# Memory values' second half ahead of attention, other fillers in the router, and the overflow branch one expert earlier

## The chip, the cores and the metric

The kernel runs on one core of one Trainium2 chip. The metric is the time of one execution on the device in microseconds (us), the median of three runs. A profiled execution of the same program gives the trace.

## What is computed

Two transformer blocks over 256 tokens of width 1024, in fp32. Cut to what matters here:

```python
x = x + g1 * mixed                              # block 1: latent attention and neighbourhood attention
hx2 = modulate(rmsnorm(x, norm_ffn_g), sh2, sc2)
x = x + g2 * hierarchical_moe(hx2, ...)         # 4 groups, 16 experts: one group, then two experts of it
x = rmsnorm(x, final_norm_g)
...
kv = mem_n @ w_mem_kv                           # block 2: keys and values of 256 memory tokens
k, v = jnp.split(kv, 2, axis=-1)
...
x = x + merged @ w_out
x = x + jnp.square(jax.nn.relu(h2 @ w_up)) @ w_down
```

The memory's keys and values depend on the input alone, so they can be computed at any time before block 2's cross attention.

## The kernel before

**Products.** The big weights are read once, as pieces of up to 1 MB (128 partitions x 2048 numbers). A product is made of three fp32r matmuls: a weight piece is split by ScalarE (line 207, the high part; each fourth by VectorE) and VectorE (line 208, the rest). `Stream` holds the jobs in order; `step` runs one split piece and prepares the next ones. The loads stand in one list, `plan`, and SP issues them in that order through `pump`, as tiles of SBUF come free. Tiles are handed out by `take` and handed back by `give`, first in, first out: who takes a tile waits for its last user.

**Stages around the change.** The projections of block 1 end with the job `J_nv` (the neighbourhood attention's values). The attention begins with scores of the neighbourhood heads, then the two halves of w_uq and of w_ukv; short matmuls, softmax on VectorE and ScalarE, and ROPE on GpSimd alternate. In it, line 859 in `router_const` multiplies the shift of the norm by the router's weights. The output projection `J_wo` adds to x; behind its second half stands the router.

**Router.** x is transposed by TensorE (`xa_T`, line 1037 on; an instruction of it has the helper's line 531), the logits come from the transposed x (line 1049), the norm's factor r2 from sums of squares. VectorE ranks groups and experts by comparisons of all pairs (lines 1117 to 1126) and TensorE counts each token's slot in its expert (lines 1131 to 1133). D, a 0/1 matrix of tokens by slots for four experts, follows (line 1143). `gather` (line 1181) multiplies the normalized tokens, split into xh and xlo, by D, four experts at a time, into `xg`. The normalized token is kept in `xn`; xh is ScalarE's rounding of it and xlo GpSimd's difference. While the router waits, TensorE runs pieces of `J_mv[1]`, the second half of the memory values: `fill(n)` runs n pieces of 6 matmuls (line 252), 8 pieces in all; its result goes through the tile `mvt` to DRAM (`mvd`), from which block 2 reads it.

**MoE.** 16 experts, 64 slots each. `moe_up` multiplies by gate and up weights (line 1269), `moe_down(e - 2)` follows two experts later (line 1303), and `moe_comb(p)` adds a pair of experts to the four banks of the output (line 1328). Tokens without a slot are the matter of `beyond()`, a branch that all engines pass: each loads a flag, and jumps over the branch's body when no token was left out, as with these inputs. It stands behind the down product of expert 12. The residual x is added to the four banks by `add_x` behind the last experts.

Of the kernel before, what the change touches and what calls it, by code (L numbers as in the profile page):

```python
# [9 lines left out]
F32 = mybir.dt.float32  # L10
# [11 lines left out]
NE = 16  # L22
# [67 lines left out]
def body(tc, d, out, dbg=None, stop=None):  # L90
# [87 lines left out]
    class Stream:  # L178
# [62 lines left out]

        def fine(self, job):

            while self.pos < job.end:
                job, key, a, k, kg, first, last, done = self.g[self.pos]
                s = self.prepared.pop(self.pos)
                if first:
                    job.accs = job.acc()
                for m, (hi, lo) in enumerate(job.lhs):
                    for kk in range(kg):  # L250
                        for j, (x, w) in enumerate(((hi, 0), (lo, 0), (hi, 1))):
                            T.matmul(job.accs[m], x(k + kk), s[:, w, kk, :], start=first and kk == 0 and j == 0,  # L252
                                     stop=last and kk == kg - 1 and j == 2)
                    if last:
                        job.evac(m, job.accs[m])
                    if m == len(job.lhs) - 1:
                        give(s)
                        self.pos += 1
                    yield

        def step_w(self, job, s, k, kg, first, last):
# [330 lines left out]
    J_mk = [Job(P_memk[c], 512, mlhs, ev_memk(c)) for c in range(2)]  # L592
    J_mv = [Job(P_memv[c], 512, mlhs, ev_memv(c), acc=(lambda: [bank(), bank()]) if c else None) for c in range(2)]
    for j in J_mk + J_mv[:1]:
# [159 lines left out]
    J_nv = Job(P_nv, 512, al, ev_nv)  # L754
    for j in (J_kvl, J_ql, J_nq, J_nk, J_nv):
        S.add(j)
# [110 lines left out]
    def latents():  # L867
# [36 lines left out]
        give(st["kvl"], st["kvT"])  # L904
        router_const()

# [93 lines left out]
    J_wo = [Job(P_wo[c], 512, wol, ev_wo(c)) for c in range(2)]  # L1000
    for j in J_wo + J_mv[1:]:
        S.add(j)
# [32 lines left out]
    def xa_T(c):  # L1035
        for k0, bk in transposed_pairs(lambda tt, k: x[:, tt, 512 * c + k:512 * c + 512:4], 4):
# [22 lines left out]

    xres = x  # L1060
# [7 lines left out]
    mvt[1] = take([128, 2, 512], F32, "mvt")  # L1068
    mvg = S.fine(J_mv[1])

    def fill(n):
        for _ in range(n):
            next(mvg, None)

    fill(3)
    give(oTh, oTl, gb[0])
# [6 lines left out]
    r2 = rstd_of(ss2t, 1024, "r2")  # L1083
    fill(2)
    logits(1, 0)
    logits(1, 1)
    give(xaT)
    keep(4)
    xn = take([128, 2, 1024], F32, "xn2")
    xh = take([128, 2, 1024], F32R, "xh")  # L1090
    xlo = take([128, 2, 1024], F32R, "xlo")
    keep(1)
    def fo(t):
        return t.rearrange("p (h j q) -> p h j q", h=2, j=4)

    def fi(t):
        return t.rearrange("p (h q j) -> p h j q", h=2, j=4)

    V.tensor_scalar(fo(xn[:, 0, :]), fi(x[:, 0, :]), r2[:, 0:1], None, op0=OP.mult)
# [9 lines left out]
    keep(1)  # L1109

# [55 lines left out]
    def halves(n):  # L1166
        hi, lo = take([128, 2, 1024], F32R, "xh"), take([128, 2, 1024], F32R, "xlo")
        for tt in range(2):
            A.activation(hi[:, tt], xn[:, tt], AF.Copy)
            G.tensor_tensor(lo[:, tt], xn[:, tt], hi[:, tt].bitcast(F32), op=OP.subtract)  # L1170
        xh_[n] = hi, lo

    def gather(n):

        xh, xlo = xh_[n]
        Dn = [D[n][:, tt].rearrange("p e c -> p (e c)") for tt in range(2)]
        for q in range(2):
            bks = [bank() for _ in range(2)]
            for i, (h, tt) in enumerate(((xh, 0), (xh, 1), (xlo, 0), (xlo, 1))):
                for k in range(4):  # L1180
                    T.matmul(bks[k // 2][:, 256 * (k % 2):256 * (k % 2) + 256],
                             h[:, tt, (4 * q + k) * 128:(4 * q + k + 1) * 128], Dn[tt],
                             start=(i == 0 and k % 2 == 0), stop=(i == 3), skip_group_check=True)
            for k in range(4 * q, 4 * q + 4):
                bk = bks[(k % 4) // 2][:, 256 * (k % 2):256 * (k % 2) + 256]
                if k in (0, 1, 4, 6):
                    V.tensor_scalar(xg[n][:, k], bk, a2[:, k:k + 1], sh2[:, k:k + 1], op0=OP.mult, op1=OP.add)
                else:
                    A.activation(xg[n][:, k], bk, AF.Identity, scale=a2[:, k:k + 1], bias=sh2[:, k:k + 1])
            yield  # L1190
# [131 lines left out]
    def moe_comb(p):  # L1322
        for dh in range(2):
            for tt in range(2):
                if p == 0:
                    yb[tt][dh] = bank("acc")
                for w in range(2):
                    T.matmul(yb[tt][dh], DT[:, (2 * dh + tt) * 128:(2 * dh + tt + 1) * 128], RB[:, w, dh, :],
                             start=(p == 0 and w == 0), stop=(p == 7 and w == 1), skip_group_check=True)

# [71 lines left out]
    def beyond():  # L1402
        flag = nc.values_load(over[0:1, 0:1], min_val=0, max_val=1)
        with tc.If(flag > 0, label="over"):  # L1404
            hb = take([128, 2, 512], F32, "hb")
            xb = take([128, 2, 1024], F32, "xb")
# [8 lines left out]
            give(xb)  # L1415
            hbT = take([128, 4, 256], F32, "hbT")
            for e in range(NE):
# [26 lines left out]
                give(*wd)  # L1444
            give(hb, hbT, h2T)
        A.preload_act_table_set("silu_and_others")

    for e in range(NE):
        if e == NE - 2:
            tc.mark_branch_hint_location("over", "LikelyTaken", engines=[mybir.EngineType.PE])  # L1450
        if e == NE - 3:
# [5 lines left out]
        if e == 1:  # L1457
            lim[:] = [99, 2]
        p = e // 2
        if e % 2 == 0:  # L1460
            if e and e % 4 == 0:
# [23 lines left out]
        else:  # L1485
            moe_up(e, 0, 4)
            if e == 1:
                gm = take([128, 4, 512], F32, "gm")
                bcast_rows(1, gm)
# [12 lines left out]
        if e % 4 == 3:  # L1502
# [3 lines left out]
            pump()  # L1506
        if e == NE - 2:
            beyond()
# [5 lines left out]
        if e == 12:  # L1514
            junk[0] = cp.tile([128, 1024], BF, name="junkB", tag="junk")
            give(xn)
            lim[:] = [99, 0]
# [385 lines left out]
```

## Time and profile before

| | |
|---|---|
| median of 3 runs | 1071.27 us (1068.0 to 1072.09) |
| profiled execution, its own time | 1069.21 us |
| its span (first to last instruction) | 1067.4 us |
| mean granted clock of TensorE | 0.992 of full |
| TensorE busy | 1037.5 us, 97% |
| VectorE, ScalarE, GpSimd busy | 593.8, 437.4, 92.4 us |
| read from DRAM | 249.7 MB |

The 1.8 us between the span and the execution's time lie around the program. The profile's times in order of the program count from the span's start. A busy share of TensorE includes overlapping instructions, so the time that a group of matmuls needs is read from the start of its first to the start of what follows.

### The profile page before, as it was taken

To read this page: it belongs to the slowest core of one execution; us is meant where nothing else is said; L and a number is where in the kernel's file an instruction comes from. 1 tells how busy PE (TensorE), PEld (TensorE's weight loads), DVE (VectorE), ACT (ScalarE), POOL (GpSimd) and SP (SyncE) were. 2 spreads that over 40 slices of the span, in tenths; PEclk is the share of its full clock that TensorE was granted. 3 is DMA by queue.
4 is the path that set the end of the run, shared out by engine and by line. 5 is a ranking of instruction groups with operands and counts; after the bars stand their busy time and mean duration, and the time that the engine had idled before them with its cause. 6 is when DMAs were issued, how large, how long until landed. Compare 5 with 4: busy or idle time off the path is not lost.

```text
span 1067.4 us, 14961 instructions
## 1 busy us (share of the span) xinstructions
PE 1037.5 (97%) x6035; PEld 777.6 (73%) x6035; DVE 593.8 (56%) x928; ACT 437.4 (41%) x744; POOL 92.4 (9%) x100
## 2 busy tenths in 40 slices
PE   6999999999999999998999999999999999999998
PEld 5587866657744343433699789998888889999996
DVE  5565237775624342523666556766456677666544
ACT  5664115674423131312534684444443144443332
POOL 0000303000201010100104452000000000000000
PEclk9999999999999999999999999999999999999999
DMA  9999741625789999999924324537566555455511
GB/s 333 402 354 346 222 150 54 251 105 240 273 344 419 418 419 420 419 419 412 383 70 160 129 78 151 175 119 260 174 204 229 197 197 197 160 196 201 193 41 40
DMA packets 82410, 254.95 MB, mean 239 GB/s; under 512 B 4760, under 2 KB 8344, under 8 KB 67616
## 3 DMA queue, kind: packets, MB, share of 16 engines
q1 hardware_dynamic: 80848, 249.22, 62.7%
q0 software_dynamic: 1488, 4.72, 1.4%
q8 instruction: 49, 0.80, 0.3%
q14 instruction: 25, 0.20, 0.1%
HBM read 249.73 MB, written 4.19 MB: 238 GB/s over the span
## 4 chain that ended last, share of the span: by engine, by line
PE 73%; DMA 19%; DVE 4%; ACT 2%; SPq 1%; issue 1%; DVEq 0%; ACTq 0%
PE acc L233 35%; PE acc L272 14%; DMA raw<-in_w_up 9%; PE b L272 8%; DMA raw<-in_w_down 6%; PE b L1269 3%; PE b L531 2%; DMA raw<-in_w_mod 2%; PE b L640 2%; DMA raw<-in_w_in 1%; PE acc L964 1%; PE b L252 1%; SPq L141 1%; DVE split L208 1%; DVE sm L940 1%; PE b L1610 1%
## 5 line engine op out<-in xcount | busy, mean ns | idle before, releaser
L208 DVE TENSOR_TENSOR split<-raw,split 128x1024 fp32r<-128x1024 f32 (+2 forms) x226 | 267.8, 1212 | 92.7 <-ACT split L207 90.5
L207 ACT ACTIVATE split<-raw 128x1024 fp32r<-128x1024 f32 (+2 forms) x170 | 168.7, 1034 | 63.0 <-DMA raw<-in_w_uq 15.7
L272 PE MATMUL acc<-uh,split 128*128 128x256 f32 x640 | 123.2, 288 | 1.4 <-ACT uh L546 1.4
L1269 PE MATMUL b<-raw,xg 128*64 128x512 f32 x512 | 116.1, 602 | 3.8 <-DVEq L1404 3.8
L272 PEld LDWEIGHTS acc<-uh,split 128*128 128x128 f32 x640 | 102.5, 193 | 2.7 <-ACT uh L546 1.8
L233 PE MATMUL acc<-split,uh 128*128 128x512 f32 x320 | 101.3, 392 | 0.0
L272 PE MATMUL b<-fh,split 128*128 128x256 f32 x512 | 93.8, 283 | 0.3 <-DVE split L208 0.3
L272 PE MATMUL acc<-ul,split 128*128 128x256 f32 x320 | 91.3, 285 | 0.1
L233 PE MATMUL acc<-split,hidT 128*128 128x512 f32 x384 | 88.4, 389 | 0.0
L1269 PEld LDWEIGHTS b<-raw,xg 128*64 128x64 f32 x512 | 35.8, 138 | 71.7 <-issue 69.9
L233 PEld LDWEIGHTS acc<-split,hidT 128*128 128x128 f32 x384 | 71.6, 188 | 14.6
L272 PEld LDWEIGHTS b<-fh,split 128*128 128x128 f32 x512 | 80.4, 192 | 0.8 <-DVE split L208 0.5
L272 PE MATMUL b<-fl,split 128*128 128x256 f32 x256 | 72.4, 283 | 0.0
L233 PEld LDWEIGHTS acc<-split,uh 128*128 128x128 f32 x320 | 60.1, 188 | 12.8
L272 PEld LDWEIGHTS acc<-ul,split 128*128 128x128 f32 x320 | 61.9, 193 | 0.7 <-DVE ul L547 0.6
L233 PE MATMUL acc<-split,ul 128*128 128x512 f32 x160 | 62.3, 390 | 0.0
L1303 PE MATMUL b<-raw,RA 128*64 128x512 f32 x256 | 58.5, 596 | 1.2 <-DMA raw<-in_w_down 1.2
L1317 DVE SCALAR_TENSOR_TENSOR RA<-b,wc,gm 64x512 f32<-64x512 f32 x32 | 24.0, 750 | 60.4 <-PE b L1303 59.9
L1318 ACT ACTIVATE RB<-RA 64x512 fp32r<-64x512 f32 x32 | 20.1, 628 | 77.6 <-DVE RA L1317 77.5
L272 PEld LDWEIGHTS b<-fl,split 128*128 128x128 f32 x256 | 49.1, 192 | 0.3
L1830 ACT ACTIVATE hid<-b 128x512 f32<-128x512 f32 x16 | 9.5, 595 | 91.3 <-PE b L272 91.3
L1303 PEld LDWEIGHTS b<-raw,RA 128*64 128x64 f32 x256 | 17.8, 137 | 37.6 <-issue 32.2
(414 smaller groups left out, 1738.7 us busy)
## 6 DMA issues: line engine op xcount, KB each, us to landing
raw<-in_w_up SPq DMA_DIRECT2D x48, 1024.0 KB, 13.2
raw<-in_w_down SPq DMA_DIRECT2D x48, 1024.0 KB, 16.2
raw<-in_w_in SPq DMA_DIRECT2D x46, 1024.0 KB, 7.5
raw<-in_w_gate SPq DMA_DIRECT2D x32, 1024.0 KB, 19.8
raw<-in_w_mod SPq DMA_DIRECT2D x24, 1024.0 KB, 8.2
raw<-in_w_out SPq DMA_DIRECT2D x8, 1024.0 KB, 6.1
raw<-in_w_mem_kv SPq DMA_DIRECT2D x7, 1024.0 KB, 11.1
raw<-in_w_conv_out SPq DMA_DIRECT2D x4, 1024.0 KB, 5.1
```

The source lines that it names most:

```text
L141: nc.sync.dma_start(t, src)
L207: A.activation(s[:, 0], src, AF.Copy)
L208: V.tensor_tensor(s[:, 1], src, s[:, 0].bitcast(F32), op=OP.subtract)
L233: T.matmul(job.accs[m], x(k + kk), s[:, w, kk, :], start=job.start and first and kk == 0 and j == 0, stop=job.stop and last and kk == kg - ...
L252: T.matmul(job.accs[m], x(k + kk), s[:, w, kk, :], start=first and kk == 0 and j == 0, stop=last and kk == kg - 1 and j == 2)
L272: T.matmul(bk[:, o:o + 256], s[:, w, kk, 128 * b:128 * b + 128], x(k + kk), start=first and b % per == 0 and r == 0 and kk == 0 and j == 0 ...
L531: T.transpose(bk[0:m, i * 128:i * 128 + p], s, ident)
L640: T.matmul(modacc[Tn][32 * g:32 * g + 32, :], cond[:, k, :], w[:, g // 2, 512 * (g % 2):512 * (g % 2) + 512] if Tn == 2 else w[:, g, :], s ...
L1269: T.matmul(b[64 * j:64 * j + 64, :], lt, raw((nm, e, k // 4))[:, k % 4, :], start=(k == 0), stop=(k == 7), skip_group_check=True)
L1303: T.matmul(b[64 * j:64 * j + 64, :], t[:, k, :], raw(("d", e, k // 2))[:, k % 2, 512 * dh:512 * dh + 512], start=(k == 0), stop=(k == 3), ...
L1317: V.scalar_tensor_tensor(RA[r, dh, :], b[r, :], wc[r, dh, e % 2:e % 2 + 1], gm[r, dh], op0=OP.mult, op1=OP.mult)
L1318: A.activation(RB[r, 0, dh, :], RA[r, dh, :], AF.Copy)
```

## The change

1. `J_mv[1]` runs whole behind `J_nv`, and its two loads stand before those of w_uq; the write of `mvd` follows at once. `fine` and `fill` are gone.
2. `router_const` stands behind `J_wo[1]` in the router. The other fillers there are two of the four additions of x, which now begin their banks, and `bcast_rows(1, gm)`, the broadcast of the gate row to all partitions, before in expert 1. `xa_T` transposes one half of the tokens after the other.
3. `xn` is gone. xh is made from x and r2 with its columns as they lie, xlo by VectorE in one operation from x, r2 and xh; the gather reads every fourth column as its stationary operand. The first gather runs all parts of xh before those of xlo, and takes its four banks at once.
4. `beyond()` stands behind `moe_comb(5)`, in expert 13. Two of its tiles become one.

```diff
+    P_memv.append(plan_w(("mv", 1), d["w_mem_kv_2"], 1024, 1536, 512))
     P_uq = [plan_w(("uq", c), d["w_uq"], 384, 384 * c, 384) for c in range(2)]
...
-    P_memv.append(plan_w(("mv", 1), d["w_mem_kv_2"], 1024, 1536, 512))
...
+    mvt[1] = take([128, 2, 512], F32, "mvt")
+    S.run(J_mv[1])
+    G.dma_start(mvd[:, :, 512:1024], mvt[1])
+    give(memTh, memTl, mvt[1])
...
         give(st["kvl"], st["kvT"])
-        router_const()
...
-    def add_x(tt, dh):
-        T.matmul(yb[tt][dh], ident, xres[:, tt, 512 * dh:512 * dh + 512], start=False, stop=False, skip_group_check=True)
+    def add_x(tt, dh, first=False):
+        if first:
+            yb[tt][dh] = bank("acc")
+        T.matmul(yb[tt][dh], ident, x[:, tt, 512 * dh:512 * dh + 512], start=first, stop=False, skip_group_check=True)
...
     S.run(J_wo[1])
-    fill(3)
+    router_const()
...
-    fill(2)
-    logits(1, 0)
-    logits(1, 1)
+    add_x(0, 0, True)
+    logits(1, 0, 1)
...
-    for tt in range(2):
-        A.activation(fo(xh[:, tt]), fi(x[:, tt, :]), AF.Identity, scale=r2[:, tt:tt + 1])
-    A.activation(fo(xn[:, 1, :]), fi(x[:, 1, :]), AF.Identity, scale=r2[:, 1:2])
-    for tt in range(2):
-        G.tensor_tensor(xlo[:, tt], xn[:, tt], xh[:, tt].bitcast(F32), op=OP.subtract)
+    def x_hi(hi):
+        for tt in range(2):
+            A.activation(hi[:, tt], x[:, tt, :], AF.Identity, scale=r2[:, tt:tt + 1])
+    def x_lo(hi, lo):
+        for tt in range(2):
+            V.scalar_tensor_tensor(lo[:, tt], x[:, tt, :], r2[:, tt:tt + 1], hi[:, tt].bitcast(F32), op0=OP.mult, op1=OP.subtract)
+    x_hi(xh)
...
+    add_x(1, 0, True)
+    bcast_rows(1, gm)
...
-    fill(1)
...
     slots_of(0)
+    x_lo(xh, xlo)
     tot = smal([128, 16], "tot")
     V.tensor_reduce(tot, bl[:, 32:64].rearrange("p (t e) -> p e t", t=2), AX.X, OP.add)
...
-                             h[:, tt, (4 * q + k) * 128:(4 * q + k + 1) * 128], Dn[tt],
+                         h[:, tt, 512 * q + k:512 * q + 512:4], Dn[tt],
...
-    fill(8)
-    G.dma_start(mvd[:, :, 512:1024], mvt[1])
-    give(memTh, memTl, mvt[1])
...
-        if e == NE - 2:
+        if e == NE - 3:
             beyond()
...
-    add_x(0, 0)
+    add_x(0, 1)
     moe_down(NE - 2)
-    add_x(1, 0)
     moe_down(NE - 1)
-    add_x(0, 1)
     add_x(1, 1)
```

The order of SP's loads at the end of the projections, before and now (each `raw` tile is a piece of weights, the DRAM tensor stands behind the arrow):

```order
L141 DMA raw_1383<-in_w_uq 128x3x384
L141 DMA raw_1474<-in_w_uq 128x3x384
L141 DMA raw_1521<-in_w_ukv 128x2x512
L141 DMA raw_1540<-in_w_ukv 128x2x512
L141 DMA raw_2015<-in_w_out 128x4x512
```

```order
L141 DMA raw_1383<-in_w_mem_kv 128x4x512
L141 DMA raw_1453<-in_w_mem_kv 128x4x512
L141 DMA raw_1472<-in_w_uq 128x3x384
L141 DMA raw_1474<-in_w_uq 128x3x384
L141 DMA raw_1491<-in_w_ukv 128x2x512
L141 DMA raw_1525<-in_w_ukv 128x2x512
```

The two pieces of w_mem_kv take the first two places, and the four of the attention follow them.

ScalarE at the start of the attention, before and now, with what each instruction waits for (`nv` is the end of the projections, `P` the softmax's exponential, `split` the high part of a weight piece, `q` the queries; a DMASW semaphore is one of GpSimd's DMAs):

```order
L745 ACTIVATE nv_1308<-acc_1314 128x512 [waits PE_49]
L941 ACTIVATE P_150_1456,sm<-b_1461,sm 128x512 [waits DMAHW3_49,DVE_49,Activation_49]
L207 ACTIVATE split_1476<-raw_1474 128x768 [waits DMAHW6_49]
L760 ACTIVATE q_1473<-acc_1479,rq_r 128x384 [waits PE_49]
L760 ACTIVATE q_1473<-acc_1480,rq_r 128x384 [waits PE_49]
```

```order
L726 ACTIVATE nv_1308<-acc_1314 128x512 [waits PE_49]
L207 ACTIVATE split_1455<-raw_1453 128x1024 [waits DMAHW6_49,DMAHW3_49,DVE_49]
L207 ACTIVATE split_1493<-raw_1472 128x768 [waits DMAHW7_49]
L207 ACTIVATE split_1508<-raw_1472 128x384
L570 ACTIVATE mvt_1452<-acc_1458,rmem 128x512 [waits PE_49]
L570 ACTIVATE mvt_1452<-acc_1459,rmem 128x512 [waits PE_49]
L925 ACTIVATE P_162_1532,sm<-b_1537,sm 128x512 [waits DVE_49,Activation_49]
L207 ACTIVATE split_1550<-raw_1474 128x768 [waits DMAHW0_49,DMASW2_49,Activation_49]
L741 ACTIVATE q_1549<-acc_1553,rq_r 128x384 [waits PE_49]
```

The split of the second piece of w_uq now waits for a DMA of GpSimd's as well, the write of `mvd` from `mvt`.

TensorE at the branch, before and now (`TENSOR_LOAD over` loads the flag, the body lies between the compare and the unconditional branches):

```order
L1303 MATMUL b_3618<-raw_3475,RA_2659 64x512 [waits DMAHW4_49]
L1303 MATMUL b_3618<-raw_3475,RA_2659 64x512 x3
L1403 TENSOR_LOAD over [waits DVE_49]
L1404 COMPARE_AND_BRANCH
...
L1404 UNCONDITIONAL_BRANCH [waits PE_49]
L1269 MATMUL b_5000<-raw_3494,xg_3422 64x512 [waits DVE_49,DMAHW6_49,PE_49,Activation_49]
```

```order
L1322 MATMUL acc_2831<-RB_2691,DT 128x512 x2
L1322 MATMUL acc_2834<-RB_2691,DT 128x512 x2
L1397 TENSOR_LOAD over [waits DVE_49]
L1398 COMPARE_AND_BRANCH
...
L1398 UNCONDITIONAL_BRANCH [waits PE_49]
L1263 MATMUL b_4944<-raw_3372,xg_3423 64x512 [waits DVE_49,DMAHW7_49,PE_49,Activation_49]
```

Ahead of the branch there now stand the matmuls of `moe_comb(5)`, not those of a down product.

## Rows read from the trace of the kernel before

**Rows 1.** Page, part 1: busy time of the engines, their shares and instructions.

```profile
PE 1037.5 (97%) x6035; PEld 777.6 (73%) x6035; DVE 593.8 (56%) x928; ACT 437.4 (41%) x744; POOL 92.4 (9%) x100
```

**Rows 2.** Busy time by stretch: length, engines, PEclk, DMA share, GB/s.

```profile
288.56:295.20 6.64, 6.64 (x19) 5.48 (x20) 2.08 (x10) 2.41 (x4) 2.06 (x1) 0.50 0.26 106
295.20:298.98 3.78, 3.78 (x33) 3.65 (x31) 1.11 (x3) 1.71 (x3) 0.68 (x1) 0.98 0.68 223
298.98:483.23 184.25, 183.08 (x917) 74.37 (x916) 65.12 (x121) 41.79 (x67) 14.52 (x6) 1.00 1.01 416
483.23:486.99 3.76, 0.00 (x1) 0.03 (x1) 2.87 (x4) 2.35 (x3) 0.00 (x0) 0.94 1.00 412
```

**Rows 3.** TensorE in order of time, projections and attention: start, us, instructions [idle].

```profile
154.72 0.50 PE L233 MATMUL acc<-split,hc 128*128 128x512 f32 x1
160.39 1.06 PE L640 MATMUL b<-raw,cond 128*32 128x512 f32 x8
162.45 6.97 PE L233 MATMUL acc<-split,qlT 128*128 128x384 f32 x36
171.42 5.30 PE L233 MATMUL acc<-split,kvT 128*128 128x512 f32 x22 [0.30 <-DVE split L208]
...
205.74 1.86 PE L859 MATMUL acc<-wr,sh 128*128 128x20 f32 x16
```

**Rows 4.** Landing times of the transfers with mvd, DMA share later.

```profile
DMA to landing us min/median/max: 4.7/7.5/9.2
173.00:190.00 17.00, 15.09 (x95) 10.54 (x95) 14.78 (x35) 12.35 (x30) 5.11 (x16) 1.00 0.00 0
```

**Rows 5.** Page, part 5: the splits' subtraction, over the whole program.

```profile
L208 DVE TENSOR_TENSOR split<-raw,split 128x1024 fp32r<-128x1024 f32 (+2 forms) x226 | 267.8, 1212 | 92.7 <-ACT split L207 90.5
```

**Rows 6.** VectorE and GpSimd in order of time, in the router.

```profile
273.44 2.36 DVE L208 TENSOR_TENSOR split<-raw,split 128x1024 fp32r<-128x1024 f32 x2 [1.26 <-ACT split L207]
277.76 0.69 DVE L994 TENSOR_TENSOR raw<-raw,gb 128x512 f32<-128x512 f32 x1
284.88 1.92 DVE L1117 TENSOR_TENSOR cmp<-lg 128x160 f32<-128x160 f32 x1
286.72 0.31 DVE L1118 TENSOR_TENSOR cmp<-lg 128x160 f32<-128x160 f32 x1
290.28 0.90 DVE L1143 TENSOR_TENSOR D<-cst,posm 128x512 fp32r<-128x512 f32 x1
...
284.22 2.40 POOL L1104 TENSOR_TENSOR xlo<-xn,xh 128x1024 fp32r<-128x1024 f32 x1 [4.79 <-ACT xh L1101]
```

**Rows 7.** TensorE in order of time, in the router.

```profile
278.86 1.12 PE L531 MATMUL b<-cst,raw 128*128 128x128 f32 x8
279.73 0.47 PE L252 MATMUL b<-split,memTh 128*128 128x512 f32 x1
282.57 1.85 PE L1049 MATMUL acc<-wr,xaT 128*128 128x20 f32 x16
288.56 0.61 PE L1131 MATMUL b<-selm,cst 128*128 128x32 f32 x2 [2.64 <-DVE selm L1126]
```

**Rows 8.** Weight loads of transposes: ns min/median/max, then first and last start.

```profile
L531 PEld LDWEIGHTS b<-cst,raw x8: 197/211/212, 278.6 to 279.6; 128*128 128x128 f32 x8
...
L531 PEld LDWEIGHTS b<-cst,xn x16: 139/140/142, 54.5 to 66.2; 128*128 128x128 f32 x16
```

**Rows 9.** TensorE in order of time, expert 1.

```profile
309.43 1.13 PE L981 MATMUL b<-grow,ones 1*128 1x512 f32 x4
```

**Rows 10.** TensorE in order of time, around the overflow branch.

```profile
471.80 3.65 PE L1269 MATMUL b<-raw,xg 128*64 128x512 f32 x16
486.99 5.09 PE L1269 MATMUL b<-raw,xg 128*64 128x512 f32 x16 [3.76 <-DVEq L1404]
```

**Rows 11.** Page, part 5: the down products' matmuls.

```profile
L1303 PE MATMUL b<-raw,RA 128*64 128x512 f32 x256 | 58.5, 596 | 1.2 <-DMA raw<-in_w_down 1.2
```

**Rows 12.** TensorE in order of time, the first additions of x behind expert 14.

```profile
507.65 1.13 PE L1063 MATMUL acc<-raw,cst 128*128 128x512 f32 x2
```

More of the change, by code (lines that the diff above doesn't have):

```diff
@@ L240, in step @@
             self.pos += 1
[L242 to L259, printed above, removed]
         def step_w(self, job, s, k, kg, first, last):
@@ L592, in body @@
     J_mk = [Job(P_memk[c], 512, mlhs, ev_memk(c)) for c in range(2)]
-    J_mv = [Job(P_memv[c], 512, mlhs, ev_memv(c), acc=(lambda: [bank(), bank()]) if c else None) for c in range(2)]
+    J_mv = [Job(P_memv[c], 512, mlhs, ev_memv(c)) for c in range(2)]
     for j in J_mk + J_mv[:1]:
@@ L754, in body @@
     J_nv = Job(P_nv, 512, al, ev_nv)
-    for j in (J_kvl, J_ql, J_nq, J_nk, J_nv):
+    for j in (J_kvl, J_ql, J_nq, J_nk, J_nv, J_mv[1]):
         S.add(j)
@@ L1000, in body @@
     J_wo = [Job(P_wo[c], 512, wol, ev_wo(c)) for c in range(2)]
-    for j in J_wo + J_mv[1:]:
+    for j in J_wo:
         S.add(j)
@@ L1035, in xa_T @@
     def xa_T(c):
-        for k0, bk in transposed_pairs(lambda tt, k: x[:, tt, 512 * c + k:512 * c + 512:4], 4):
+        bks = [bank() for _ in range(2)]
+        for tt in range(2):
+            for k in range(4):
+                o = 256 * (k % 2) + 128 * tt
+                T.transpose(bks[k // 2][:, o:o + 128], x[:, tt, 512 * c + k:512 * c + 512:4], ident)
+        for k0 in (0, 2):
+            bk = bks[k0 // 2].rearrange("p (k t) -> p k t", k=2)
             for kk in range(2):
@@ L1067, in body @@
     la[0] = 2
[L1068 to L1073, printed above, removed]
-    fill(3)
+    router_const()
     give(oTh, oTl, gb[0])
@@ L1167, in halves @@
         hi, lo = take([128, 2, 1024], F32R, "xh"), take([128, 2, 1024], F32R, "xlo")
-        for tt in range(2):
-            A.activation(hi[:, tt], xn[:, tt], AF.Copy)
-            G.tensor_tensor(lo[:, tt], xn[:, tt], hi[:, tt].bitcast(F32), op=OP.subtract)
+        x_hi(hi)
+        x_lo(hi, lo)
         xh_[n] = hi, lo
@@ L1176, in gather, with part, evac @@
         Dn = [D[n][:, tt].rearrange("p e c -> p (e c)") for tt in range(2)]
[L1177 to L1181, printed above, removed]
-                             h[:, tt, (4 * q + k) * 128:(4 * q + k + 1) * 128], Dn[tt],
-                             start=(i == 0 and k % 2 == 0), stop=(i == 3), skip_group_check=True)
+        def part(q, bks, i):
+            h, tt = (xh, xh, xlo, xlo)[i], i % 2
+            for k in range(4):
+                T.matmul(bks[k // 2][:, 256 * (k % 2):256 * (k % 2) + 256],
+                         h[:, tt, 512 * q + k:512 * q + 512:4], Dn[tt],
+                         start=(i == 0 and k % 2 == 0), stop=(i == 3), skip_group_check=True)
+        def evac(q, bks):
             for k in range(4 * q, 4 * q + 4):
@@ L1189, in gather @@
                     A.activation(xg[n][:, k], bk, AF.Identity, scale=a2[:, k:k + 1], bias=sh2[:, k:k + 1])
+        if n == 0:
+            bq = [[bank(), bank()] for _ in range(2)]
+            for i in range(3):
+                for q in range(2):
+                    part(q, bq[q], i)
+            for q in range(2):
+                part(q, bq[q], 3)
+                evac(q, bq[q])
+            return
+        for q in range(2):
+            bks = [bank(), bank()]
+            for i in range(4):
+                part(q, bks, i)
+            evac(q, bks)
             yield
-    fill(8)
-    G.dma_start(mvd[:, :, 512:1024], mvt[1])
-    give(memTh, memTl, mvt[1])
     xg[0] = take([128, 8, 256], F32, "xg")
@@ L1324, in moe_comb @@
             for tt in range(2):
-                if p == 0:
+                if p == 0 and dh:
                     yb[tt][dh] = bank("acc")
@@ L1328, in moe_comb @@
                     T.matmul(yb[tt][dh], DT[:, (2 * dh + tt) * 128:(2 * dh + tt + 1) * 128], RB[:, w, dh, :],
-                             start=(p == 0 and w == 0), stop=(p == 7 and w == 1), skip_group_check=True)
+                             start=(p == 0 and w == 0 and dh == 1), stop=(p == 7 and w == 1), skip_group_check=True)
     late = None
@@ L1404, in beyond @@
         with tc.If(flag > 0, label="over"):
-            hb = take([128, 2, 512], F32, "hb")
+            hbb = take([128, 2048], F32, "hb")
+            hb = hbb[:, 0:1024].rearrange("p (t n) -> p t n", t=2)
+            hbT = hbb[:, 1024:2048].rearrange("p (k t) -> p k t", k=4)
             xb = take([128, 2, 1024], F32, "xb")
@@ L1444, in beyond @@
                 give(*wd)
-            give(hb, hbT, h2T)
+            give(hbb, h2T)
         A.preload_act_table_set("silu_and_others")
     for e in range(NE):
-        if e == NE - 2:
-            tc.mark_branch_hint_location("over", "LikelyTaken", engines=[mybir.EngineType.PE])
         if e == NE - 3:
@@ L1459, in body @@
         p = e // 2
+        if e == NE - 3:
+            tc.mark_branch_hint_location("over", "LikelyTaken", engines=[mybir.EngineType.PE])
         if e % 2 == 0:
```

16 lines of the change are left out of this document (3 added, 13 removed).

## The prediction

> **What bounds the kernel now.** I read the page first, for the busy shares of the engines. TensorE is busy 97% of the span [rows 1], so nearly all that it executes is time, and what can still be won lies in single places where it stands or runs slowly. [...] Last I read the order in time of TensorE, VectorE, ScalarE and GpSimd around each place that the change touches; these rows are named below.
>
> The profiled execution took 1069.21 us (span 1067.4), the median of the three runs is 1071.27. I make the sum on the profiled execution and take its result off the median.
>
> **The change, part by part.**
>
> *Memory values, second half, moved ahead of attention.* The 48 matmuls of 128x512 were fillers in the router, and now stand whole behind the neighbourhood values. One step of that job before it, 24 such matmuls, goes from 154.72 to 160.39, 5.67 us [rows 3]; two steps make **+11.3**. That they come in time is likely: their two loads take the places of the two w_uq loads on SP's queue, which are moved behind them and still have 11 us of new matmuls to land in.
>
> *A new wait at the start of attention.* The result is written to DRAM by GpSimd directly behind, and the tile that it is written from is the next to be handed out: ScalarE's split of the second half of w_uq waits for that write (the order of ScalarE in the section on the change shows it), and behind it in ScalarE's queue stand the softmax and the other splits. TensorE has the four matmuls of scores and 18 of 128x384 to do meanwhile; 36 took 6.97 us [rows 3], so 18 take 3.5, and with the scores (1.1) it is out of work 4.6 us after the last memory matmul. One operation on a piece of 1024 columns takes 1.2 us [rows 5]. ScalarE's last copy into the tile has 512 columns, so the write starts about 0.8 behind that matmul, and after it lands the split and its subtraction, of 768 columns each, take some 1.8. With a landing of L the stall is 0.8 + L + 1.8 - 4.6 = L - 2.0. The trace has no write of this size on idle DMA engines. Its three transfers of this tile landed in 4.7, 7.5 and 9.2 us [rows 4]; 4.7 is a read of two such halves, the two writes ran beside weight loads, and here the DMA engines are idle (0.00 from 173 to 190 [rows 4]). I take L = 4, a little under the shortest, so 2.0 less the 0.3 that it stands there now [rows 3]: **+1.7**; bounds are half of 4.7 and the whole of 9.2, so 0 and +7. [...]
>
> *The router's constant* (8 products of 128x20) leaves the attention, where it occupies 1.86 us of TensorE [rows 3]; some of that will be filled by waits for the softmax: **-1.5** (0 to -1.8). It now runs while the router waits for x, and costs nothing there.
>
> *The router, 274.77 to 298.98, 24.2 us.* It loses 11 us of fillers, but they covered waits, so what is left is a chain. VectorE could begin the last half of x only after two subtractions for the memory weights (273.44 + 2.36), and x was complete at 278.45 [rows 6]; without them x comes some 2.0 earlier. From the transposes (278.86) to the logits (282.57) lie 3.7 us [rows 7], of which the queued fillers made about 1.5. The first comparison of the ranks takes 1.92, its twin of the same shape 0.31; it ends 0.1 us behind GpSimd's first subtraction of x_lo (284.22 + 2.40 [rows 6]), with which it seems to have stood in line. GpSimd does no more subtractions, so I take 1.5 off. Then the three small products and D, 2.6 us (288.56 to 290.28 + 0.90 [rows 6, 7]), as now. New is that the fourth accumulator bank of the gather is the one whose totals VectorE reads behind both x_lo operations; at the price of the split's subtraction (1212 ns) two of them are 2.4 us, and the gather stands some 1.9 us for it. The gather's 32 matmuls themselves keep 3.8. Added up: logits done at about 280.5, ranks 283, D 285.4, gather 291.1, first expert 291.6, which is 16.8 us. The longest wait within is under 2 us, where 2.64 stood before the clock fell [rows 7], yet there are four of 1 to 2 us and few fillers, so I let a quarter of the price of the lower clock stand (3.8 us, the gather's matmuls at half the pace): 17.8, **-6.4**. The bounds are 15.9 (half of the wait for the totals) and 20.6 (all of the price): -8.3 to -3.6.
>
> *Strided weights of the gather.* Without a kept normalized token, x_hi and x_lo are contiguous and the gather reads every fourth column as stationary operand, 4 x 32 matmuls. A weight load with that stride took 211 ns in the transposes of x, one without it 140 [rows 8], but the eight strided transposes advanced one per 0.109 us (278.86 to 279.73 [rows 7]), faster than the gather's 0.115 (33 in 3.78 [rows 2]): the load lies beside the running matmul. I take **0**; if each 71 ns showed, it would be +9.1. [...]
>
> *Six more operations of x_lo on VectorE, in the MoE*, 1.2 us each: it is busy 65 of 184 us there [rows 2], so nothing. *The broadcast of the gate row* leaves expert 1: **-1.1** [rows 9].
>
> *The branch.* Behind the down product of expert 12, TensorE waited 3.76 us until VectorE had finished with that product and gone through the branch, and the next 16 matmuls took 5.09 us instead of 3.6 [rows 10]: 5.3 together. Now it stands behind the combination that ends at 471.80 [rows 10], which reads only what VectorE finished before, and no product stands between that and the branch: the wait is the passage alone, which I estimate at 0.7 to 0.9 (VectorE is busy 2.87 of the 3.76 us [rows 2]), and the clock stays. **-4.6** (-2 to -5). SP now has three w_down loads behind the branch; they go out some 2 us late with seven others in flight, and are needed 20 us later.
>
> *Waits for w_down in the MoE*, 1.2 us [rows 11]: with two memory loads fewer in the way and four more weight loads in attention, the loads run some 4 us ahead, TensorE less: **-1.2**. *The tail* loses two of four additions of x, 1.13 for two [rows 12]: **-1.1**.
>
> Sum: 11.3 + 1.7 - 1.5 - 6.4 - 1.1 - 4.6 - 1.2 - 1.1 = -2.9; 1071.27 - 2.9 = **1068.4 us**.
>
> **Rivals.**
> - *The router keeps its full clock* (-1.9), and the write is at its lower bound (-1.7): -2.9 - 3.6 = -6.5, **1064.8**. For it: no wait as long as 2.64. Against: the clock fell in this very place.
> - *The write takes 9.2* as its twin did: TensorE stands 7.2 us in place of 2, and the next matmuls run at half clock as behind the branch (1.5): -2.9 + 6.7 = +3.8, **1075.1**, slower than before. It decides from a landing of 6.9 on. Against: no loads run beside it.
> - *Strided loads show* in the gathers: -2.9 + 9.1 = +6.2, **1077.5**. It decides when over 22 ns of each 71 show.
> - *The change wins nothing in the MoE*, because the loads set its end: then the down product of expert 13 ends when it does now, and only the tail's 1.1 is left, **1070.2**. Against: SP's queue gets two loads out of the way.
>
> **How the numbers follow.** Forecast 0.52, full clock 0.22, slow write 0.10, loads 0.10, strided 0.06. A measurement can tell 0.5%, 5.4 us, from no change. Faster by that needs under 1065.9: most of the full-clock case (0.17) and a tenth of chance from the forecast's lower bounds: 0.26. Slower needs over 1076.6: strided (0.05) and the worst of the slow write (0.03): 0.08. Same: 0.66. The range leaves out the strided case and the extremes of the full-clock case and of the slow write: 1062.5 to 1075.5.
>
> **What would show it.** Attention starts 11.3 us later; ScalarE's split of w_uq waits for the DMA of mvd, and TensorE some 2 us for it. The router lasts 16 to 20 us, with a first comparison of 0.3 us. The MoE starts near 304, the gathers keep 3.8 us, the gap at the branch is under 1 us, no clock of 0.5 follows it, and no w_down is waited for. The forecast is wrong if the stall at attention's start exceeds 5 us, if a gather takes 5, or if the branch still costs 3.

## The result, and the profile after

The changed kernel takes 1076.12 us (median of 6 runs, 1075.4 to 1078.01) against 1070.68 (6 runs): 1.0055 of the time before, with a 95% interval of 1.0041 to 1.0069. I had forecast 1068.4, in a range of 1062.5 to 1075.5: the time went the other way.

The page of the kernel after, part 1, as in [rows 1]:

```profile
PE 1046.7 (97%) x6035; PEld 790.4 (74%) x6035; DVE 600.6 (56%) x935; ACT 433.9 (40%) x743; POOL 73.5 (7%) x92
```

TensorE is 9.2 us longer busy and GpSimd 18.9 us shorter. From the starts of the first instructions of each stage on TensorE, in the two profiled executions:

| stage on TensorE | before, us | after, us | difference |
|---|---|---|---|
| start to the end of `J_nv` and its modulation | 161.39 | 162.30 | +0.9 |
| memory values | - | 11.11 | +11.1 |
| attention and output projection | 113.38 | 112.53 | -0.85 |
| router, to the first expert | 24.21 | 19.35 | -4.9 |
| first expert to expert 14's first matmul | 172.82 | 180.62 | +7.8 |
| from there to block 2's first projection | 48.04 | 40.53 | -7.5 |
| block 2 | 547.56 | 547.86 | +0.3 |
| span | 1067.4 | 1074.3 | +6.9 |

The first and last row I take for differences between executions, since the program does the same there. Of the other five, three have the sign of the forecast. The attention, with the new wait in it and the router's constant out, should have become 0.2 us longer and became 0.85 shorter; the last sections come back to it. The large miss is the MoE up to expert 14: it should have become some 2 us shorter and became 7.8 longer. Its stretch holds three gathers, four experts apart. The second gather before, and after (TensorE in order of time; the four transposes between the halves belong to another step):

```profile
338.03 1.08 PE L1181 MATMUL b<-D,xh 128*128 128x256 f32 x8
338.94 1.07 PE L1181 MATMUL b<-D,xlo 128*128 128x256 f32 x8
339.86 0.65 PE L1294 MATMUL b<-cst,gm 128*128 128x128 f32 x4
340.26 1.56 PE L1181 MATMUL b<-D,xh 128*128 128x256 f32 x8
341.66 1.07 PE L1181 MATMUL b<-D,xlo 128*128 128x256 f32 x8
342.57 0.25 PE L1242 MATMUL b<-cw,RA 128*128 128x6 bf16 x4
```

```profile
343.15 1.93 PE L1161 MATMUL b<-D,xh 128*128 128x256 f32 x8
344.92 2.05 PE L1161 MATMUL b<-D,xlo 128*128 128x256 f32 x8
346.80 0.66 PE L1288 MATMUL b<-cst,gm 128*128 128x128 f32 x4
347.22 2.11 PE L1161 MATMUL b<-D,xh 128*128 128x256 f32 x8
349.16 2.03 PE L1161 MATMUL b<-D,xlo 128*128 128x256 f32 x8
351.03 0.25 PE L1236 MATMUL b<-cw,RA 128*128 128x6 bf16 x4
```

Without the transposes it was 4.1 us and is 7.5: eight matmuls took 0.92 us (1.40 in one of the four groups) and take 1.8 to 1.9. Three gathers at +3.3 make +10. The weight loads of x_lo in all gathers (one line for each kernel: ns min/median/max, then first and last start), before and after:

```profile
L1181 PEld LDWEIGHTS b<-D,xlo x64: 187/188/192, 296.1 to 446.8; 128*128 128x128 f32 x64
```

```profile
L1161 PEld LDWEIGHTS b<-D,xlo x64: 329/332/336, 301.3 to 461.6; 128*128 128x128 f32 x64
```

They grew from 188 to 332 ns. The other places, first the start of the attention (TensorE), with the landing times of the three transfers of `mvd`:

```profile
173.41 1.13 PE L910 MATMUL b<-nkT,nqT 64*128 64x512 f32 x4
174.47 3.39 PE L233 MATMUL acc<-split,qlT 128*128 128x384 f32 x18
178.59 0.61 PE L233 MATMUL acc<-split,qlT 128*128 128x384 f32 x2 [0.73 <-ACT split L207]
179.58 3.04 PE L233 MATMUL acc<-split,qlT 128*128 128x384 f32 x16 [0.38 <-DVE split L208]
...
184.66 5.28 PE L233 MATMUL acc<-split,kvT 128*128 128x512 f32 x22 [0.32 <-DVE split L208]
```

```profile
DMA to landing us min/median/max: 3.1/4.8/7.3
```

TensorE waits 0.73 and 0.38 us for the split, and the 0.3 us of before, for the split behind it, are still there. The write of the second half is the transfer of 3.1 us. The router, VectorE and then TensorE (the rows that answer to [rows 6, 7]), and three stretches of it with their clock:

```profile
291.84 0.33 DVE L1098 TENSOR_TENSOR cmp<-lg 128x160 f32<-128x160 f32 x1
...
295.64 0.69 DVE L1123 TENSOR_TENSOR D<-cst,posm 128x512 fp32r<-128x512 f32 x1
296.25 2.47 DVE L1082 SCALAR_TENSOR_TENSOR xlo<-raw,r_r,xh 128x1024 fp32r<-128x1024 f32 x2
```

```profile
296.48 1.75 PE L1161 MATMUL b<-D,xh 128*128 128x256 f32 x6 [1.10 <-DVE D L1123]
298.98 2.70 PE L1161 MATMUL b<-D,xh 128*128 128x256 f32 x10 [0.74 <-DVE tot L1129]
301.48 3.89 PE L1161 MATMUL b<-D,xlo 128*128 128x256 f32 x16
305.29 4.94 PE L1263 MATMUL b<-raw,xg 128*64 128x512 f32 x22
```

```profile
285.94:292.00 6.06, 6.06 (x45) 5.08 (x43) 4.07 (x15) 3.62 (x9) 0.68 (x1) 1.00 1.01 424
292.20:293.30 1.10, 1.10 (x5) 0.30 (x4) 1.03 (x4) 1.06 (x2) 0.00 (x0) 0.88 0.98 413
293.90:294.80 0.90, 0.87 (x5) 0.90 (x5) 0.00 (x0) 0.83 (x2) 0.00 (x0) 0.50 1.03 428
```

The first comparison takes 0.33 us where it took 1.92, the gather waits 1.10 us for D and 0.74 for the totals, and the clock falls between 292.2 and 293.3, before the slots are counted (from 293.93 on). The branch, and the waits of the down products (as [rows 10, 11]):

```profile
485.91 3.65 PE L1263 MATMUL b<-raw,xg 128*64 128x512 f32 x16 [0.40 <-PEq L1398]
```

```profile
L1297 PE MATMUL b<-raw,RA 128*64 128x512 f32 x256 | 57.7, 594 | 0.0
```

The wait at the branch is 0.40 us in place of 3.76, and no w_down is waited for.

### The profile page after: what moved, and what is told of

Same layout as the page of the kernel before. It is cut to its first block, busy times and chain, and to the rows that moved or that the text cites. A ratio compares the mean times of both kernels' runs of the same rounds, so it can differ in the third digit from the quotient of the medians.

```text
span 1074.3 us, 14944 instructions
## 1 busy us (share of the span) xinstructions
PE 1046.7 (97%) x6035; PEld 790.4 (74%) x6035; DVE 600.6 (56%) x935; ACT 433.9 (40%) x743; POOL 73.5 (7%) x92
## 4 chain that ended last, share of the span: by engine, by line
PE 52%; DMA 1%; DVE 1%; ACT 1%; issue 0%; DVEq 0%; ACTq 0%
PE acc L233 26%; PE acc L253 11%; PE b L253 8%; PE b L1263 1%; DMA raw<-in_w_in 1%; PE b L512 1%; PE b L1600 1%; PE b L1622 1%; PE b L1678 1%; PE b L1702 1%; PE b L1297 1%; PE b L1633 0%; PE b L1621 0%; DVE split L208 0%; ACT junkB L505 0%
## 5 line engine op out<-in xcount | busy, mean ns | idle before, releaser
L233 PE MATMUL acc<-split,memTh 128*128 128x512 f32 x128 | 43.4, 410 | 1.5 <-DVE split L208 1.3
## 6 DMA issues: line engine op xcount, KB each, us to landing
raw<-in_w_down SPq DMA_DIRECT2D x48, 1024.0 KB, 11.3
raw<-in_w_mem_kv SPq DMA_DIRECT2D x7, 1024.0 KB, 11.1
```

Source lines behind the costliest of these rows:

```text
L233: T.matmul(job.accs[m], x(k + kk), s[:, w, kk, :], start=job.start and first and kk == 0 and j == 0, stop=job.stop and last and kk == kg - ...
```

## The experiments

"Before" in each is the kernel before, run on the same chip.

### The gather alone: the layout in the kernel before, and the layout undone in the kernel after

The first puts only the strided gather into the kernel before:

```diff
-    V.tensor_scalar(fo(xn[:, 0, :]), fi(x[:, 0, :]), r2[:, 0:1], None, op0=OP.mult)
+    V.tensor_scalar(xn[:, 0, :], x[:, 0, :], r2[:, 0:1], None, op0=OP.mult)
     for tt in range(2):
-        A.activation(fo(xh[:, tt]), fi(x[:, tt, :]), AF.Identity, scale=r2[:, tt:tt + 1])
+        A.activation(xh[:, tt], x[:, tt, :], AF.Identity, scale=r2[:, tt:tt + 1])
...
-                             h[:, tt, (4 * q + k) * 128:(4 * q + k + 1) * 128], Dn[tt],
+                             h[:, tt, 512 * q + k:512 * q + 512:4], Dn[tt],
```

> The kernel before, with only the layout changed: x_hi, x_lo and the normalized token lie in x's own order, and the gather reads every fourth column as its stationary operand. Strided weight load: each gather takes 3.3 us more, 10 us in the MoE and up to 3.5 more in the router, so 1080 to 1084 against 1070.7. Rival, that the load lies beside the matmul and something else of the change costs the time: within 2 us of the kernel before.

Measured: 1080.87 us against 1068.83, ratio 1.0111 (1.0092 to 1.013): +12.0 us for this layout alone, more than the whole loss, and as expected. Its weight loads:

```profile
L1181 PEld LDWEIGHTS b<-D,xh x64: 307/329/337, 296.4 to 459.7; 128*128 128x128 f32 x64
```

In the profiled execution the four gathers take 13.5 us more (3.6 and three times 3.3). The layout does two things beside: TensorE, being later, waits for no w_down any more (1.2 us in [rows 11]), and ScalarE, which reads x as it lies, makes each x_hi in 1142 ns in place of 2126, so that GpSimd's two subtractions in the router now run one behind the other. VectorE's second comparison, 0.31 us in [rows 6], then takes 2.46 and ends 0.2 us behind the second subtraction:

```profile
283.88 4.76 POOL L1104 TENSOR_TENSOR xlo<-xn,xh 128x1024 fp32r<-128x1024 f32 x2 [3.82 <-ACT xh L1101]
```

```profile
286.36 2.46 DVE L1118 TENSOR_TENSOR cmp<-lg 128x160 f32<-128x160 f32 x1
```

The second takes the kernel after and puts the permuted layout back, in which ScalarE and VectorE read x with the stride (VectorE in two operations for each half of the tokens):

```diff
-            A.activation(hi[:, tt], x[:, tt, :], AF.Identity, scale=r2[:, tt:tt + 1])
+            A.activation(fo(hi[:, tt]), fi(x[:, tt, :]), AF.Identity, scale=r2[:, tt:tt + 1])
...
-                         h[:, tt, 512 * q + k:512 * q + 512:4], Dn[tt],
+                         h[:, tt, (4 * q + k) * 128:(4 * q + k + 1) * 128], Dn[tt],
```

> The changed kernel, with only the layout of x_hi and x_lo put back to the permuted one, so that the gather's stationary operand is contiguous again; ScalarE and VectorE now read x with the stride. Theory of the strided weight load (329 ns against 188, and 1.9 us per 8 gather matmuls against 0.92): the gathers go back to 3.7 to 4.2 us, the stretch from the first expert to expert 13's combination loses 9 to 10 us of its 178.1, and the time falls from 1076 to 1062 to 1066. Rival, that VectorE's x_lo or the order of the loads stretched the MoE: the gathers' weight loads fall back, but the stretch stays above 175 and the time above 1072. Second rival, that the loads of the expert weights set the end of the MoE once the gathers are quick: TensorE waits for w_down by 3 us or more, and the time is 1067 to 1070.

Measured: 1073.85 us against 1068.83, ratio 1.004 (1.0022 to 1.0058). The weight loads are back and the time is not (the kernel after stood at 1.0055, 1.0041 to 1.0069); neither my theory's 1062 to 1066 nor a rival came out. The instructions of the gather's operands, and then the waits of TensorE (in total, times, longest):

```profile
L1169 PEld LDWEIGHTS b<-D,xh x64: 186/188/338, 297.4 to 458.4; 128*128 128x128 f32 x64
...
L1089 DVE SCALAR_TENSOR_TENSOR xlo<-raw,r_r,xh x16: 1115/1150/1183, 297.2 to 448.2; 128x512 fp32r<-128x512 f32 x16
L1084 ACT ACTIVATE xh<-raw,r_r x8: 2102/2194/2222, 292.0 to 444.8; 128x1024 fp32r<-128x1024 f32 x8
```

```profile
PE acc L1330 <- ACT DT L1258: 4.9, 3, 1.7
...
PE b L1169 <- DVE tot L1137: 2.6, 1, 2.6
```

The stride was only handed on: VectorE takes 1150 ns for 512 columns and ScalarE 2194 for 1024, so the first gather waits 2.6 us for the totals behind x_lo, and three combinations wait 4.9 us for a copy of ScalarE's. ScalarE is not busy ahead of that copy: it stands 3.7 to 3.8 us for VectorE, which has first waited for x_hi and then been at x_lo, as here ahead of the last of the three waits:

```profile
444.96 4.39 DVE L1089 SCALAR_TENSOR_TENSOR xlo<-raw,r_r,xh 128x512 fp32r<-128x512 f32 x4 [1.50 <-ACT xh L1084]
```

This shows what the kept normalized token was for: in it the stride was paid once, and each later x_hi was a copy of 1050 ns.

### How the price depends on the distance of the columns

Two more layouts of x_hi and x_lo in the kernel after: one in which the gather reads every second column, 8 bytes apart, and one with every eighth, 32 bytes apart. For the first, ScalarE and VectorE read x in pairs of neighbouring columns, two of every four; for the second they read it as it lies.

```diff
-                         h[:, tt, 512 * q + k:512 * q + 512:4], Dn[tt],
+                         h[:, tt, 512 * q + 256 * (k // 2) + k % 2:512 * q + 256 * (k // 2) + 256:2], Dn[tt],
```

```diff
-                         h[:, tt, 512 * q + k:512 * q + 512:4], Dn[tt],
+                         h[:, tt, 4 * q + k:1024:8], Dn[tt],
```

> The changed kernel with x_hi and x_lo laid out so that the gather reads every second column (8 bytes apart) in place of every fourth (16 bytes). [...] Rival, that every stride is paid alike: 329 ns and 1076. Third possibility, cost in proportion to the distance: about 235 ns, gather pace about 0.15 us per matmul, 1067 to 1070.

> The changed kernel with x_hi and x_lo laid out so that the gather reads every eighth column (32 bytes apart). [...] If the cost grows with the distance: load over 450 ns, pace over 0.35, time over 1090.

Measured, one run each: 1065.38 and 1077.41 us, against a median of 1068.83 before. The weight loads, every second column first:

```profile
L1169 PEld LDWEIGHTS b<-D,xh x64: 193/196/331, 295.5 to 450.0; 128*128 128x128 f32 x64
```

```profile
L1169 PEld LDWEIGHTS b<-D,xh x64: 312/338/342, 296.7 to 461.0; 128*128 128x128 f32 x64
```

So 188 ns at distance 1, 196 at 2, 329 at 4, 338 at 8: nearly free at 8 bytes, the whole price at 16, and no more to speak of at 32. Neither one price for every stride nor a price in proportion to the distance fits the four figures; what makes the step between 8 and 16 bytes, no run shows.

The layout with every second column was then timed:

> The kernel with every second column, timed beside the others. If the stride of the gather's weights is the whole of what I missed, the change with that one repair is faster than before by 3 to 6 us (1063 to 1066 where before is 1069 to 1071).

Measured: 1066.74 us against 1068.68, ratio 0.9987 (0.9971 to 1.0002). With the stride repaired the change is 1.9 us ahead of before, not to be told from no change, and 9.4 us ahead of the change as it was (their chips differ). My sum, which has no price for the stride in it, -2.9, lies just inside the interval (-3.1 to +0.2). The 3 to 6 us that I expected here were too many.

### The waits of the change

```diff
-    give(memTh, memTl, mvt[1])
+    give(memTh, memTl)
...
-        give(st["kvl"], st["kvT"])
+        give(st["kvl"], st["kvT"], mvt[1])
...
     slots_of(0)
-    x_lo(xh, xlo)
     tot = smal([128, 16], "tot")
     V.tensor_reduce(tot, bl[:, 32:64].rearrange("p (t e) -> p e t", t=2), AX.X, OP.add)
     V.tensor_reduce(cm, tot, AX.X, OP.max)
+    x_lo(xh, xlo)
```

> Every second column, and two waits of the change taken away: the totals are read ahead of x_lo on VectorE (the gather's fourth bank waited 1.1 us for them), and the tile of the memory values' write is handed back at the end of the attention, so that ScalarE's split of w_uq has another tile (TensorE waited 0.7 and 0.4 us). Theory: both were on the path, 1.5 to 2 us less than with every second column alone. Rival: the gather then waits for x_lo instead, and with one tile fewer a weight load comes later: within 0.7 us of it.

Measured: 1062.83 us against 1068.68, ratio 0.9945 (0.9924 to 0.9967), and in a second set 1062.05 against 1069.11, 0.9928 (0.9906 to 0.9951). TensorE in that version, at the start of the attention and in the first gather:

```profile
177.74 3.08 PE L233 MATMUL acc<-split,qlT 128*128 128x384 f32 x16 [0.17 <-DVE split L208]
```

```profile
294.65 3.75 PE L1169 MATMUL b<-D,xh 128*128 128x256 f32 x16 [1.09 <-DVE tot L1136]
298.20 2.40 PE L1169 MATMUL b<-D,xlo 128*128 128x256 f32 x16
300.98 5.37 PE L1271 MATMUL b<-raw,xg 128*64 128x512 f32 x24 [0.38 <-DVE xg L1177]
```

The wait for the write is gone (0.17 us is left of 1.1). The gather still starts 1.09 us late. The row names the totals, but these stand only 0.1 us behind D on VectorE, which is not ready sooner:

```profile
293.82 0.69 DVE L1131 TENSOR_TENSOR D<-cst,posm 128x512 fp32r<-128x512 f32 x1
```

From there the gather runs without a break. From the router's constant to the first expert it is 16.9 us in this version, and 19.0 with every second column alone. In two more executions of this router, the second set's and the one with the branch put back (below), it takes 15.9; the three products of the slot counts take 0.38 us each there, where here they take 0.60 at a granted clock of 0.52 (292 to 294). What makes that difference, no run shows. So some 1 us comes from the tile and 2.1 to 3.1 from the router, where the medians differ by 3.9. This version beats both kernels.

A further one, with all four additions of x in the router:

```diff
+    add_x(0, 1, True)
+    add_x(1, 1, True)
     posm = smal([128, 2, 16], "posm")
...
-    add_x(0, 1)
     moe_down(NE - 2)
     moe_down(NE - 1)
-    add_x(1, 1)
```

> The same version, with the other two additions of x also in the router, between the slot counts and the first gather, where TensorE waits 1.1 us for D and the totals; they leave the end of the MoE. If that wait covers them: 1.0 to 1.6 us less than 1062.8, as two additions of 1.05 us together leave the tail, one of them beside a wait of 0.5 us. If they delay the gather: no difference.

> The same kernel as e5, on the chip of the two others, so that they are compared on one chip: 1061 to 1064.

Measured: 1063.07 us against 1062.05 on the same chip, no gain. Its two further additions stand in the router at the lower clock (0.50), and the gather starts behind them, at 298.23 (TensorE in order of time, then that stretch by engine, with the granted clock in the third column from the end):

```profile
295.46 3.76 PE L1053 MATMUL acc<-raw,cst 128*128 128x512 f32 x4
```

```profile
295.40:298.20 2.80, 2.80 (x6) 1.25 (x6) 2.45 (x7) 0.00 (x0) 0.00 (x0) 0.50 0.08 31
```

The four matmuls, at a granted clock of 0.50 throughout, occupy TensorE for 2.8 us, where the wait that they were to fill had 1.1.

### The branch, alone and taken back

The branch alone, in the kernel before:

```diff
-        if e == NE - 2:
+        if e == NE - 3:
             beyond()
```

> The kernel before, with only the branch moved behind expert 13's combination (and the two tiles of its body made one). Theory that TensorE's order is the limit: the wait of 3.8 us and the 1.5 us at half clock go, 4 to 5 us less than before. Rival, that the loads set the end of the MoE: what the branch loses comes back as waits for w_down, 3 us or more of them, and the time is within 1.5 us of the kernel before.

Measured: 1069.27 us against 1068.68, ratio 1.0011 (0.9997 to 1.0026): nothing, as the rival said. TensorE passes the branch in 0.41 us, and stands later for a down weight (the profiled execution, 1071.85 us, is the longest of the ten):

```profile
473.30 3.65 PE L1269 MATMUL b<-raw,xg 128*64 128x512 f32 x16 [0.41 <-PEq L1404]
...
492.58 5.41 PE L1303 MATMUL b<-raw,RA 128*64 128x512 f32 x16 [3.82 <-DMA raw<-in_w_down]
```

Behind that wait of 3.82 us 16 matmuls that take 3.60 (481.12) take 5.41. Behind the branch in the kernel before 16 took 5.09, with a granted clock of 0.50 from 487.00 to 489.00; here no row shows the clock behind the wait. And the branch put back to its old place in the version of 1062 us:

> The version with every second column, the totals first and the tile handed back late (1062.8 us), with the branch put back behind the down product of expert 12. With the memory weights loaded before the attention no w_down is waited for, so the branch's price must show here where it did not when the branch alone was moved in the kernel before: a wait of 3.7 to 3.9 us at the branch and 16 matmuls at half clock, 4 to 5.5 us more (1067 to 1068.5). Rival, that the branch's price is hidden in any case: within 1 us of that version.

Measured: 1068.04 us, 6.0 more than that version on the same chip (0.9985 of the time before, 0.9969 to 1.0), with the wait back:

```profile
488.62 6.61 PE L1271 MATMUL b<-raw,xg 128*64 128x512 f32 x16 [3.87 <-DVEq L1406]
```

With the branch in its new place the wait is 0.40 us and the 16 matmuls take 3.65, so this one place accounts for 6.4 us (the profiled execution is again the longest). So the same move is worth nothing in the one kernel and 6 us in the other. What the rows show to differ is what comes next: a wait of 3.82 us for a load in the one, none for a load in the other.

### The memory values back in the router

Every second column and the totals first, but `J_mv[1]` is the router's filler again, with 8 pieces spread over its waits:

```diff
-    S.run(J_mv[1])
...
+    router_const()
+    fill(1)
...
+    fill(1)
     logits(1, 0, 1)
...
+    fill(1)
     bl = bank()
...
+    fill(8)
+    G.dma_start(mvd[:, :, 512:1024], mvt[1])
```

> Every second column and the totals first, but the second half of the memory values back in the router as filler (8 pieces), with its loads behind those of w_out as before; all other parts of the change stay. Theory that the memory matmuls are worth more as fillers than as a block: the router from the end of the output projection to the first expert then takes 22 to 24 us in place of 18.4, the projections 11.3 less, no half clock, so 4 to 6 us less than with every second column alone. Rival: the loads, later by the two memory weights and by a router full of splits, set the end of the MoE; TensorE waits for w_down by 2 us or more, and the time is within 2 us of it.

Measured: 1070.1 us against 1068.68, ratio 1.0017 (0.9992 to 1.0042). The router itself does what I hoped: 24.1 us with the 11.3 of memory matmuls in it, TensorE busy 23.97 of 24.40 us (274.0 to 298.4) and the clock at 1.00. But a stretch of it has idle DMA engines, and the MoE pays (that stretch, then TensorE in expert 15); that the one is the cause of the other is not shown:

```profile
282.00:290.00 8.00, 8.00 (x39) 5.67 (x39) 5.18 (x16) 2.79 (x5) 0.00 (x0) 1.00 0.13 30
```

```profile
491.41 6.46 PE L1333 MATMUL b<-raw,RA 128*64 128x512 f32 x16 [4.81 <-DMA raw<-in_w_down]
```

It waits 4.81 us for a down weight. The version with the totals first, which has the memory values ahead of the attention (1062.83 on the same chip), waits for no load there. It differs in the tile `mvt[1]` too, which was worth some 1 of the 7.3 us between them.

## Why the prediction was wrong, point by point

**The step that failed** is "Strided weights of the gather": I took 0, because strided transposes advanced faster than the gather's matmuls, "the load lies beside the running matmul". The load of a transpose was no measure for a load of the gather, neither of its length nor of what is hidden. At the same stride the one grew by 71 ns, the other by 144 (188 to 332), and the gather's matmuls went from 0.115 us each to 0.235: 120 ns of the 144 show. The layout with the stride costs 12.0 us in the kernel before, over my upper bound of 9.1, which was worked out with the 71. The rival that I gave 0.06 was the case.

The busy share of the weight loads would not have warned me. It is 97% in the stretch with the first gather (3.65 of 3.78 us [rows 2]), but at the strided transposes, which advance no slower for it (0.109 us each; four without a stride took 0.44 us, 176.56 to 177.00), it is 100%:

```profile
278.86:279.73 0.87, 0.87 (x9) 0.87 (x8) 0.20 (x1) 0.41 (x2) 0.56 (x1) 1.00 1.10 367
```

**The other terms**, from the trace after:
- Memory values +11.3: 11.1. The loads came in time.
- The new wait +1.7: +1.1. The 0.3 that I took off is still there, at another split. The wait is where I said, only the landing was shorter: 3.1 us, where I had taken 4; by my own formula, L - 2.0, that is 1.1. With the tile handed back later (the version with the totals first), 0.17 us of the wait is left.
- The router's constant -1.5: about -1.0. The attention lost 0.85 with the new wait of 1.1 in it, but not by the constant alone. TensorE is busy 2.7 us less there: 1.8 is the constant's (205.74 to 207.53), and 0.9 is left for the clock, which falls in the output projection of the kernel before (0.90 from 248 to 256, row in the last section) and not in this execution (1.00 from 250 to 284). At that place, behind the four matmuls from one partition, two matmuls of 128x512 take 1.05 us in three of the eight executions with the memory values ahead of the attention whose rows show it, and 0.63 in the other five, so this part is chance. The waits for the softmax grew by 0.8.
- The router -6.4: -4.9. Up to D it went as forecast (10.4 us from its start, forecast 10.6); from there to the first expert it took 9.0 us in place of 7.2. With every second column the router takes 19.0, hardly better: the gather's matmuls need 6.9 us in place of 8.1, but waits are 0.8 longer. So the stride is mostly hidden there; what I had wrong is the granted clock, for which I charged a quarter of 3.8 us. It fell before the slots were counted and was 0.50 until 303.2, in the gather's second half. In the version with the memory values back in the router the same 32 matmuls take 4.3 us at a clock of 1.00, so its price is some 2.6. VectorE's comparison (0.33 us) is as worked out, and that GpSimd's subtractions held it up fits the first experiment, where the second comparison takes 2.46 us in place of 0.31 and ends 0.2 us behind the second of them. The totals cost 0.74 in place of 1.9, since the six matmuls ahead of them took 1.75 us at the lower clock (0.50).
- The branch -4.6: 3.76 and 5.09 us have become 0.40 and 3.65, so -4.8 (the stage's 7.5 holds the tail's additions and a wait for w_down as well). Taken back alone it is 6.0, alone in the kernel before 0: here it paid only where no load was waited for behind it. The version with the memory values back in the router waits for a load again (4.81 us), so it seems to be their move that puts the loads ahead; how far they are was not measured by itself. I had given the rival that "the loads set its end" for the whole change; it holds for the branch without the move.
- Waits for w_down -1.2: none is left. The broadcast and the tail's additions: within what two executions differ.

That the sum comes near with the stride repaired is partly luck: the router's clock cost some 1.6 us more than I charged, and the clock in the output projection, which is not in my sum, gave 0.9 back.

**The rivals.** The full clock did not come. The slow write did not either. The gain in the MoE was real, and the stride took it: from the first expert to block 2 it is 220.9 us before, 221.2 after, and 211.7 with every second column.

## What to carry to other kernels

Before an operand's layout is changed, price its load on an operation of the same kind: here neither the load of a transpose at the same stride nor the busy share of the loads told what the gather would pay, and one run with the layout alone did. A stride was paid in each layout tried, on TensorE, VectorE or ScalarE; pay it once, and try a layout that leaves two fp32 numbers side by side. The one with every second column was the cheapest here: 196 ns a weight load against 188 contiguous, 749 ns for 512 columns on VectorE against 1150 at every fourth, 770 on ScalarE against 1097 (half of 2194). And a wait taken away on the busiest engine was worth nothing here where a wait of 3.82 us for a load came behind it, so two moves that are each worth nothing alone may be worth 6 us together: here the branch alone gave 1.0011 of the time before, the repaired version without the branch 0.9985, and with it 0.9928.

## What the runs showed of the hardware that I had not expected

- A weight load of 128 fp32r columns: 188 ns contiguous, 196 at every second column, 329 at every fourth, 338 at every eighth. The load of a fp32 transpose grew from 140 at distance 1 to 211 at every fourth only.
- A comparison of 128x160 on VectorE, 0.31 us elsewhere, took 2.46 while GpSimd subtracted, and ended 0.2 us behind it (the first experiment).
- VectorE and ScalarE pay for the same stride: 1150 ns for 512 columns at every fourth, and 2194 ns for 1024, in the contiguous layout's experiment above. VectorE with two neighbours of every four (the layout with every second column) took 749, and ScalarE in the kernel after, where x is read as it lies, 1142. There VectorE took 2.47 us for two of 1024 (row above), some 620 ns for 512:

```profile
L1090 DVE SCALAR_TENSOR_TENSOR xlo<-raw,r_r,xh x16: 742/749/752, 295.3 to 438.9; 128x512 fp32r<-128x512 f32 x16
```

```profile
L1078 ACT ACTIVATE xh<-raw,r_r x8: 1132/1142/1148, 291.1 to 444.7; 128x1024 fp32r<-128x1024 f32 x8
```

- The granted clock fell from 1.00 to 0.50 while TensorE had no gap: it was busy 6.06 of 6.06 us before 292.0, 0.20 of 0.20 up to 292.2, and 1.10 of 1.10 between 292.2 and 293.3, where the clock's mean is 0.88; from 293.3 on it is 0.50. What it executed was 20 columns wide, a transpose, or from one partition, with only four matmuls of 128x512 among it. With memory matmuls among these the clock stayed at 1.00 (8.00 of 8.00 us busy). In the kernel before I had put the fall in the router down to the gap of 2.64 us; here it fell without one. That kernel's output projection shows the same: no gap, and a clock that is 1.00 in 16 attention products and four matmuls from one partition (249.90 to 253.84) and 0.63 behind them (253.84 to 256.00).

```profile
248.00:256.00 8.00, 8.00 (x35) 4.73 (x34) 2.12 (x3) 3.31 (x5) 0.00 (x0) 0.90 0.57 229
```

Which of these kinds of work brings the fall, the rows don't tell.
